# A batched matrix product on one core: leaner engine programs, and loads with wider source runs

## The chip, the cores and the metric

One core of a Trainium2 chip. Times are device microseconds (us). A profile is one further look at one execution, with its own time.

## The reference

```python
batch, m, k, n = 16, 512, 768, 1024
x: (batch, k, m) float32;  y: (batch, k, n) float32
out = np.einsum('bkm,bkn->bmn', x, y).astype(np.float32)
```

Each batch reads 1.5 MiB of x and 3 MiB of y and writes 2 MiB. Over 16 batches that is 109 MB (millions of bytes).

## The kernel before

SP issues all transfers from one queue. Two input buffers (`xs`, `ys`) alternate; VectorE (DVE) casts them to bf16, TensorE (PE) multiplies, ScalarE (ACT) moves PSUM to one of five output buffers, and SP stores with a lag of four batches. What lets a load start:

```python
    LAG = 4
    NO = 5
    # ... buffers, semaphores ...
    @block.sync
    def _(sync):
        def store(b):
            sync.wait_ge(outs, b + 1)
            sync.dma_start(o_v[b], ob[b % NO][:]).then_inc(so[b % NO], 16)

        for b in range(B):
            i = b % 2
            if b >= 2:
                sync.wait_ge(cast, b - 1)          # casts of batch b-2 are done
            sync.dma_start(xs[i][:], x_v[b]).then_inc(sx[i], 16)
            sync.dma_start(ys[i][:], y_v[b]).then_inc(sy[i], 16)
            if b >= LAG:
                store(b - LAG)
        # ... the last four stores, waits for all stores ...

    @block.vector
    def _(vector):
        for b in range(B):
            # ... wait for xs, cast x; wait for ys, cast y in two halves ...
            vector.drain().then_inc(cast, 1)

    def batch(tensor, i, first):                   # PE, cut
        for mo in range(MT):                       # MT = 4, 12 matmuls each
            tensor.wait_ge(room, 1).then_inc(room, -1)
            # ... matmuls into ps[mo]; before the 4th of them: wait for y's second half
            mm.then_inc(groups, 1)
    # ACT: one copy per mo (128 x 1024), a drain per batch that counts `outs`
```

## Time and profile before

| | before |
|---|---|
| median of runs | 262.83 us (262.77 to 262.95) |
| span of the profile | 261.2 us |
| DMA engines' busy share | 98.1% |
| PE busy | 72% |

The page, the start of the timeline and the tail are shown in the prediction. DMA issues (KB each, then median us from issue to landing):

```profile
ys<-in_y_dram SPq DMA_DIRECT2D x16, 3072.0 KB, 27.7
out_dram<-ob SPq DMA_DIRECT2D x16, 2048.0 KB, 32.1
xs<-in_x_dram SPq DMA_DIRECT2D x16, 1536.0 KB, 20.8
```

A load of x takes 20.8 us to land although its bytes need only 3.7 (3.66 us from the median engine's end of the transfer before to its end of this one): the rest is time in the queue behind other transfers. That reading is a median over 16 loads. The waits of the SP queue (total, times, longest):

```profile
SPq L72 <- DVEq L94: 188.5, 14, 15.5
```

SP spends most of its time, 188.5 of 261.2 us, waiting for the casts before it may issue a load. That alone says nothing of a loss: the DMA engines are busy for 98.1% of the span all the same.

### The profile page before, as it was taken

To read this page: it belongs to the slowest core of one execution; us is meant where nothing else is said; L and a number is where in the kernel's file an instruction comes from. 1 tells how busy PE (TensorE), PEld (TensorE's weight loads), DVE (VectorE), ACT (ScalarE), POOL (GpSimd) and SP (SyncE) were. 2 spreads that over 40 slices of the span, in tenths; PEclk is the share of its full clock that TensorE was granted. 3 is DMA by queue.
4 is the path that set the end of the run, shared out by engine and by line. 5 is a ranking of instruction groups with operands and counts; after the bars stand their busy time and mean duration, and the time that the engine had idled before them with its cause. 6 is when DMAs were issued, how large, how long until landed. Compare 5 with 4: busy or idle time off the path is not lost. (4 is left out here: it accounts for less than half of the span.)

```text
span 261.2 us, 1938 instructions
## 1 busy us (share of the span) xinstructions
PE 188.0 (72%) x768; PEld 87.1 (33%) x768; DVE 83.0 (32%) x48; ACT 66.1 (25%) x65; POOL 0.2 (0%) x4
## 2 busy tenths in 40 slices
PE   0039999998948949398595997939678394896920
PEld 0014555443513515144152342514334142342500
DVE  0261734435223252322524214252132523225000
ACT  1003343433331314114032140412314033131410
POOL 0000000000000000000000000000000000000000
PEclk9999999999986999979798697997999899797995
DMA  7999999999999999999999999999999999999993
GB/s 265 431 425 427 438 411 453 425 386 418 446 420 439 420 430 446 415 441 420 439 437 412 447 423 440 415 432 442 423 434 420 435 433 423 440 433 421 434 421 141
DMA packets 6915, 109.09 MB, mean 418 GB/s; under 512 B 768, under 2 KB 768, under 8 KB 768
## 3 DMA queue, kind: packets, MB, share of 16 engines
q1 hardware_dynamic: 6912, 109.05, 98.1%
q8 instruction: 1, 0.02, 0.0%
q14 instruction: 2, 0.02, 0.0%
HBM read 75.50 MB, written 33.55 MB: 417 GB/s over the span
## 5 line engine op out<-in xcount | busy, mean ns | idle before, releaser
L105 PE MATMUL ps<-yb,xb 128*128 128x512 bf16 x768 | 188.0, 406 | 61.6 <-PEq L100 55.9
L105 PEld LDWEIGHTS ps<-yb,xb 128*128 128x128 bf16 x768 | 87.1, 116 | 162.1 <-issue 96.7
L125 ACT COPY ob<-ps 128x1024 f32<-128x1024 f32 x64 | 64.9, 1013 | 183.6 <-PE ps L105 183.6
L93 DVE CAST yb<-ys 128x3072 bf16<-128x3072 f32 x32 | 54.9, 1757 | 88.4 <-DMA ys<-in_y_dram 88.4
L89 DVE CAST xb<-xs 128x3072 bf16<-128x3072 f32 x16 | 28.2, 1760 | 67.5 <-DMA xs<-in_x_dram 66.8
L125 ACT ACT_TABLE_LOAD x1 | 1.3, 1283 | 1.0 <-SPq L44 1.0
L142 POOL MEMSET const-uint8-127<- 128x1 uint8 x1 | 0.1, 102 | 0.0
L142 POOL MEMSET const-bfloat16-1.0<- 128x1 bf16 x1 | 0.1, 101 | 0.0
L142 POOL MEMSET const-float32-0.0<- 128x1 f32 x1 | 0.1, 98 | 0.2 <-issue 0.2
L142 POOL MEMSET const-float32-1.0<- 128x1 f32 x1 | 0.1, 98 | 0.0
## 6 DMA issues: line engine op xcount, KB each, us to landing
ys<-in_y_dram SPq DMA_DIRECT2D x16, 3072.0 KB, 27.7
out_dram<-ob SPq DMA_DIRECT2D x16, 2048.0 KB, 32.1
xs<-in_x_dram SPq DMA_DIRECT2D x16, 1536.0 KB, 20.8
```

Source lines behind the costliest of these rows:

```text
L89: nc.vector.tensor_copy(xb[i][:], xs[i][:]).then_inc(ready, 1)
L93: nc.vector.tensor_copy(yb[i][:, ks], ys[i][:, ks]).then_inc(ready, 1)
L105: mm = nc.tensor.matmul(ps[mo][:, nt], x_w[:, kt, mo], yb[i][:, kt, nt * NF:(nt + 1) * NF], start=(kt == 0), stop=(kt == KT - 1))
L125: nc.scalar.copy(ob[b % NO][:, mo].rearrange("p (t f) -> p t f", f=NF), ps[mo][:]).then_inc(room, 1)
L142: nc = _bacc.Bacc("TRN2", target_bir_lowering=False, num_devices=1)
```

## The change

Its intent: fewer instructions and barriers (no block construct, half the ACT copies, no drains per batch, `head_slot` set for PE's loop), and fewer read pieces in the loads: 32 source runs of 48 KB instead of 128 of 12 KB for x, 64 of 48 KB instead of 128 of 24 KB for y. To do without the casts' drain, loads wait for PE's groups instead.

```diff
-            if b >= 2:
-                sync.wait_ge(cast, b - 1)
-            sync.dma_start(xs[i][:], x_v[b]).then_inc(sx[i], 16)
-            sync.dma_start(ys[i][:], y_v[b]).then_inc(sy[i], 16)
+        if b >= 2:
+            nc.sync.wait_ge(groups, 2 * (b - 2) + 1)
+        wide_dma("x", xs[i][:], x_v[b], 4, True).then_inc(sx[i], 16)
+        wide_dma("y", ys[i][:], y_v[b], 2, True).then_inc(sy[i], 16)
...
-            vector.drain().then_inc(cast, 1)
...
-            sync.wait_ge(outs, b + 1)
+        if b < B - 2:
+            nc.sync.wait_ge(groups, 2 * (b + 2))
+        else:
+            nc.sync.wait_ge(outs, b - (B - 3))
...
-        for mo in range(MT):
+        for g in range(2):
             tensor.wait_ge(room, 1).then_inc(room, -1)
+            for m in range(HB):
...
             mm.then_inc(groups, 1)
...
-        with tensor.Fori(0, B // 2):
+    with nc.Fori(0, B // 2, engines=OrderedEngineSet([pe]), head_slot={pe: 0}):
...
-            for mo in range(MT):
-                nc.scalar.copy(ob[...][:, mo], ps[mo][:]).then_inc(room, 1)
-            scalar.drain().then_inc(outs, 1)
+        for g in range(2):
+            cp = nc.scalar.copy(ob[...][:, g * HB:(g + 1) * HB], ps[g][:])
+            if b < B - 1:
+                cp.then_inc(room, 1)
```

`groups` now counts half batches, two per batch, so a load of batch b waits until PE has done the first half of batch b-2.

More of the change, by code (lines that the diff above doesn't have):

```diff
@@ L3 @@
 _os.environ.setdefault("NEURON_RT_ULTRASERVER_MODE", "4")
+import copy as _copy
 from contextlib import ExitStack
@@ L10 @@
 from concourse._compat import with_exitstack
+from concourse.ordered_engine_set import OrderedEngineSet
 @with_exitstack
@@ L41 @@
     KH = KT // 2
-    GP = NT * NF
     ctx.enter_context(tc.tile_critical())
@@ L50 @@
     ob = [ec(nc.sbuf_tensor(f"ob{i}", [P, MT, N], FP32)) for i in range(NO)]
-    ps = [ec(nc.psum_tensor(f"ps{i}", [P, NT, NF], FP32)) for i in range(MT)]
+    HB = MT // 2
+    ps = [ec(nc.psum_tensor(f"ps{i}", [P, HB, NT, NF], FP32)) for i in range(2)]
     sx = [ec(nc.semaphore(f"sx{i}")) for i in range(2)]
@@ L54 @@
     so = [ec(nc.semaphore(f"so{i}")) for i in range(NO)]
-    cast = ec(nc.semaphore("cast"))
     ready = ec(nc.semaphore("ready"))
@@ L59 @@
     outs = ec(nc.semaphore("outs"))
-    block = ec(nc.Block())
-    @block.sync
-    def _(sync):
-        def store(b):
-            sync.wait_ge(outs, b + 1)
-            sync.dma_start(o_v[b], ob[b % NO][:]).then_inc(so[b % NO], 16)
-        for b in range(B):
-            i = b % 2
-            if b >= 2:
-                sync.wait_ge(cast, b - 1)
-            sync.dma_start(xs[i][:], x_v[b]).then_inc(sx[i], 16)
-            sync.dma_start(ys[i][:], y_v[b]).then_inc(sy[i], 16)
-            if b >= LAG:
-                store(b - LAG)
-        for b in range(B - LAG, B):
-            store(b)
-        for i in range(NO):
-            sync.wait_ge(so[i], 16 * len(range(i, B, NO)))
@@ L81, in _ @@
-    @block.vector
-    def _(vector):
-        for b in range(B):
-            i = b % 2
-            n = 16 * (b // 2 + 1)
-            if b >= 2:
-                vector.wait_ge(groups, MT * (b - 1))
-            vector.wait_ge(sx[i], n)
-            nc.vector.tensor_copy(xb[i][:], xs[i][:]).then_inc(ready, 1)
-            vector.wait_ge(sy[i], n)
-            for h in range(2):
-                ks = slice(h * KH, (h + 1) * KH)
-                nc.vector.tensor_copy(yb[i][:, ks], ys[i][:, ks]).then_inc(ready, 1)
-            vector.drain().then_inc(cast, 1)
@@ L96, in batch @@
-    def batch(tensor, i, first):
-        x_w = xb[i][:].rearrange("p k (j mo) -> p k mo j", mo=MT)
-        tensor.wait_ge(ready, 2).then_inc(ready, -2)
-        for mo in range(MT):
-            tensor.wait_ge(room, 1).then_inc(room, -1)
-            for nt in range(NT):
-                for kt in range(KT):
-                    if mo == 0 and nt == 0 and kt == KH:
-                        tensor.wait_ge(ready, 1).then_inc(ready, -1)
-                    mm = nc.tensor.matmul(
-                        ps[mo][:, nt], x_w[:, kt, mo],
-                        yb[i][:, kt, nt * NF:(nt + 1) * NF],
-                        start=(kt == 0), stop=(kt == KT - 1))
-            mm.then_inc(groups, 1)
@@ L111, in _ @@
-    @block.tensor
-    def _(tensor):
-        with tensor.Fori(0, B // 2):
-            batch(tensor, 0, False)
-            batch(tensor, 1, False)
-    @block.scalar
-    def _(scalar):
-        nc.scalar.nop().then_inc(room, MT)
-        for b in range(B):
-            for mo in range(MT):
-                if mo == 0 and b >= NO:
-                    scalar.wait_ge(so[b % NO], 16 * (b // NO))
-                scalar.wait_ge(groups, MT * b + mo + 1)
-                nc.scalar.copy(ob[b % NO][:, mo].rearrange("p (t f) -> p t f", f=NF),
-                               ps[mo][:]).then_inc(room, 1)
-            scalar.drain().then_inc(outs, 1)
+    made = {}
@@ new lines, in wide_dma @@
+    def wide_dma(key, dst, src, dram_rows, load):
+        if key not in made:
+            made[key] = nc.sync.dma_start(dst, src)
+            return made[key]
+        pat = mybir.BassSymbolicTensorAccessPattern
+        widen = lambda a: a.rearrange("(q r) k m -> q (r k m)", r=dram_rows)
+        plain = lambda a: a.rearrange("p k m -> p (k m)")
+        s, d = (widen(src), plain(dst)) if load else (plain(src), widen(dst))
+        return nc.sync.add_instruction(_copy.replace(
+            made[key].ins, name=nc.get_next_instruction_name(),
+            ins=(pat(ap=s.ap, dtype=s.dtype, bass_ap=s, is_dma=False),),
+            outs=(pat(ap=d.ap, dtype=d.dtype, bass_ap=d, is_dma=False),),
+            sync_info=None, ant_dge_precooked=False))
@@ new lines, in store @@
+    def store(b):
+        if b < B - 2:
+            nc.sync.wait_ge(groups, 2 * (b + 2))
+        else:
+            nc.sync.wait_ge(outs, b - (B - 3))
+        nc.sync.dma_start(o_v[b], ob[b % NO][:]).then_inc(so[b % NO], 16)
+    for b in range(B):
+        i = b % 2
+        if b >= 2:
+            nc.sync.wait_ge(groups, 2 * (b - 2) + 1)
+        wide_dma("x", xs[i][:], x_v[b], 4, True).then_inc(sx[i], 16)
+        wide_dma("y", ys[i][:], y_v[b], 2, True).then_inc(sy[i], 16)
+        if b >= LAG:
+            store(b - LAG)
@@ new lines, with batch @@
+    for b in range(B - LAG, B):
+        store(b)
+    for b in range(B):
+        i = b % 2
+        n = 16 * (b // 2 + 1)
+        if b >= 2:
+            nc.vector.wait_ge(groups, 2 * (b - 1))
+        nc.vector.wait_ge(sx[i], n)
+        nc.vector.tensor_copy(xb[i][:], xs[i][:]).then_inc(ready, 1)
+        nc.vector.wait_ge(sy[i], n)
+        for h in range(2):
+            ks = slice(h * KH, (h + 1) * KH)
+            nc.vector.tensor_copy(yb[i][:, ks], ys[i][:, ks]).then_inc(ready, 1)
+    def batch(i):
+        x_w = xb[i][:].rearrange("p k (j mo) -> p k mo j", mo=MT)
+        nc.tensor.wait_ge(ready, 2).then_inc(ready, -2)
+        for g in range(2):
+            nc.tensor.wait_ge(room, 1).then_inc(room, -1)
+            for m in range(HB):
+                for nt in range(NT):
+                    for kt in range(KT):
+                        if g == 0 and m == 0 and nt == 0 and kt == KH:
+                            nc.tensor.wait_ge(ready, 1).then_inc(ready, -1)
+                        mm = nc.tensor.matmul(
+                            ps[g][:, m, nt], x_w[:, kt, g * HB + m],
+                            yb[i][:, kt, nt * NF:(nt + 1) * NF],
+                            start=(kt == 0), stop=(kt == KT - 1))
+            mm.then_inc(groups, 1)
@@ new lines @@
+    pe = nc.tensor.engine
+    with nc.Fori(0, B // 2, engines=OrderedEngineSet([pe]), head_slot={pe: 0}):
+        batch(0)
+        batch(1)
+    nc.scalar.nop().then_inc(room, 2)
+    for b in range(B):
+        if b >= NO:
+            nc.scalar.wait_ge(so[b % NO], 16 * (b // NO))
+        for g in range(2):
+            nc.scalar.wait_ge(groups, 2 * b + g + 1)
+            cp = nc.scalar.copy(ob[b % NO][:, g * HB:(g + 1) * HB].rearrange("p m (t f) -> p m t f", f=NF),
+                                ps[g][:])
+            if b < B - 1:
+                cp.then_inc(room, 1)
+        if b == B - 2:
+            nc.scalar.drain().then_inc(outs, 1)
@@ L131 @@
+    cp.then_inc(outs, 1)
+    for i in range(NO):
+        nc.sync.wait_ge(so[i], 16 * len(range(i, B, NO)))
 _INS = ['x', 'y']
```

## The prediction

> **What bounds the kernel now.** I read the page first (busy shares, slices, DMA queues), then the timeline at the start and the end, the waits of the SP queue, fine windows over the tail, and last the single packet records of the trace.
>
> The page of the kernel before:
>
> ```profile
> span 261.2 us, 1938 instructions
> ...
> PE 188.0 (72%) x768; PEld 87.1 (33%) x768; DVE 83.0 (32%) x48; ACT 66.1 (25%) x65; POOL 0.2 (0%) x4
> ...
> DMA  7999999999999999999999999999999999999993
> ...
> q1 hardware_dynamic: 6912, 109.05, 98.1%
> q8 instruction: 1, 0.02, 0.0%
> q14 instruction: 2, 0.02, 0.0%
> ```
>
> No compute engine is above 72%, while the DMA row is 9 in every slice but the first and the last: 109.05 MB run through 16 engines that are busy 98.1% of the span. The kernel is bound by transfers from end to end; only the start, the tail, and dry spots in the queue can move the time.[...]
>
> The timeline, start:
>
> ```profile
> 0.94 0.38 SPq L72 DMA_DIRECT2D xs<-in_x_dram  x1
> ...
> 18.49 0.33 SPq L72 DMA_DIRECT2D xs<-in_x_dram  x1
> ...
> 25.00 1.01 ACT L125 COPY ob<-ps 128x1024 f32<-128x1024 f32 x1 [1.57 <-PE ps L105]
> 25.99 3.43 DVE L93 CAST yb<-ys 128x3072 bf16<-128x3072 f32 x2 [5.55 <-DMA ys<-in_y_dram]
> ```
>
> Loads of batch 2 are issued at 18.49 us, right after the casts of batch 0. The ACT copy at 25.00 is the second of batch 0: PE finishes half a batch just before it. Load 1 ends only about then (its y is seen at 25.99).
>
> Windows over the tail (columns: stretch, length, then PE, PEld, DVE, ACT, POOL busy, clock, DMA share, GB/s):
>
> ```profile
> 256.00:257.00 1.00, 0.00 (x0) 0.00 (x0) 0.00 (x0) 0.00 (x0) 0.00 (x0) 0.50 0.54 229
> 257.00:258.00 1.00, 0.00 (x0) 0.00 (x0) 0.00 (x0) 0.00 (x0) 0.00 (x0) 0.50 0.08 33
> 258.00:259.00 1.00, 0.00 (x0) 0.00 (x0) 0.00 (x0) 0.00 (x0) 0.00 (x0) 0.50 0.12 49
> 259.00:260.00 1.00, 0.00 (x0) 0.00 (x0) 0.00 (x0) 0.00 (x0) 0.00 (x0) 0.50 0.00 0
> ```
>
> Most engines are done before 257; a share of 0.08 to 0.12 is one or two of 16. The packet records say the same: of the 16 completion packets of the last store the median ends at 256.82, the last at 259.42. So one late engine sets the end, 2.6 us behind the median. Followed back by the completion packets of each transfer, the last engine is 0.75 us behind the median until about 35 us and 1.98 behind from 39 us: an instruction packet of 16 KB lies at 38.0 us and takes 1.07 us. A second engine, 1.9 late at the end, fell behind at 105 and 137 us, where no instruction packet lies.
>
> [...]median packets are 460 ns for 12 KB, 611 for 16 KB, 912 for 24 KB; 12,288 bytes more cost 452 ns, so 27.2 GB/s an engine, 435 for 16.[...] the line through those medians leaves 8 ns per packet, and successive packets overlap by about 4, so some 4 ns net.[...] here the cast of the last y starts at 235.57, although the median engine finished it at 232.45 and the last at 235.09.[...]
>
> **The change part by part.**
>
> 1. Wider source runs. Reads of x go from 128 runs of 12 KB to 32 of 48 KB, reads of y from 128 of 24 KB to 64 of 48 KB (first x and first y stay plain). The bytes, the writes and the order stay. Per engine and batch x falls from 8 read pieces to 2 and y from 8 to 4: 10 fewer. If the fixed cost goes with the read, 10 x 4 ns x 15 batches = 0.6 us; at the full 8 ns 1.2 us; if it goes with the write, nothing. I take -0.4. It can't be more: all data at 435 GB/s needs 250.6 us, and the packets without their stalls 252.7 already (254.3 of medians less 1.6 of overlap).
>
> 2. No block construct. At the start SP goes through a branch at 0.79 before its first DMA at 0.94: about -0.1. At the end SP passes its last wait at 259.80, and the block's barrier of all engines ends at 260.18, before the outer exit begins: about -0.4. Sum -0.5.
>
> 3. Fewer instructions. ACT copies go from 64 to 32, 32 per-batch drains become one[...]. If the 16 KB packet at 38 us goes or falls where it does no harm, the latest engine becomes the second latest: 2.6 to 1.9, so -0.7. I count -0.5.
>
> 4. Load waits. A load of batch b waited for the casts of batch b-2; now it waits for PE to finish half of batch b-2, about 5 to 7 us later. In steady state nothing comes of it: a load issued at 18.49, or every 15.8 us later on, has 20 us or more to landing (page: 20.8 for x, 27.7 for y), so the queue stays 10 us deep or more. But once it is too late: load 2 must wait for half of batch 0, 25.00 us instead of 18.49. The engines finish load 1 at 24.3 (first), 24.76 (median), 25.5 (last), by their completion packets. From issue to first data takes 1.0 us (0.94 to 1.95), so first data at 26.0, 25.9 with the earlier start; and the first packets out of an empty queue took 0.96 to 1.74 us instead of 0.46, 0.8 more in the mean. The median engine loses 1.1 + 0.8 = 1.9 us, the last one about 1.2. Load 3 (half of batch 1, 35.4, data at 36.4) meets a queue busy until about 26.7 + 10.9 = 37.6, and load 4 (45.7, data 46.7) one busy until 48.5: no second dry spot, and from there the stores deepen it. The pause also lines the engines up again, which takes back perhaps 0.5 of the lag. Net +1.3.
>
> 5. Stores wait for a later batch's PE groups: before store b-4, SP has already waited for a later count, so it is free. The one copy of 2,048 columns instead of two of 1,024 (1.01 us each) ends the last eviction about 0.9 us later. The last store was issued at 250.78 against a median end of the store before at 251.93; now it comes after it, so early engines wait about 0.6. The late engine, with two to three packets left, does not. From its y landing the late engine has five stores left, 5 x 4.87 = 24.3 us; the chain cast, PE, copy, issue, store is 0.5 + 2.1 + 12.05 + 1.9 + 0.9 + 4.9 = 22.4. About 2 us of slack: +0.1.
>
> Sum: -0.4 - 0.5 - 0.5 + 1.3 + 0.1 = 0.0. A second way, by the median engine: 256.82 - 0.1 - 0.4 + 1.9 = 258.2, plus a lag of 1.3 (restart spread, about half a microsecond at 55 to 58 us where all engines stall, and the stalls at 105 and 137) is 259.5, against 259.42; then 0.4 less to leave: 0.3 us faster.
>
> **Rivals.**
> - Transfers gain all they can: the wide reads save 1.2 us and smooth the stalls, and no instruction packet hits an engine (-1.5), with a mild dry spot (+0.5). Then about 260. For it: engines do stall on their own (28 packets of y at 55 to 58 us took over 1 us).[...]
> - The dry spot bites twice (loads 2 and 3), or a restart costs more than at the start: 264 to 265. For it: load 3 has only 1.2 us to spare. Against: each pause gives the next load that much more room.
> - The wide loads run badly[...]. One extra wait of 0.1 us per wide load would be 3 us over 30 loads, 266. Nothing in the trace speaks for it; both 32 and 64 divide evenly over 16.
> - Compute becomes the bound: PE is at 72%, with 55.9 us idle for inputs; two halves of PSUM give a copy of about 1.9 us a window of 5.2. No.
>
> **Range and chances.** The two sums give 0.0 and -0.3 us. The gains are more likely undersized than the loss, since someone tuned for them, so I put 261.8 us, and 259.6 to 264.2 for 8 in 10, where the ends are the first and the second rival. Over 2% faster means below 257.6, which asks that nearly all stalls vanish[...]: 0.05. Over 2% slower, above 268.1, needs the third rival: 0.04. Within 2%: 0.91.
>
> **What would show it.** Step 1: fewer packets of 48 KB, 1,816 ns each, in place of 12 and 24 KB ones; or the same counts and medians, then nothing saved. Step 2: the last landing lies about 1.4 instead of 1.8 us before the end of the span. Step 3: no instruction packet mid-run, and a late engine under 2 us behind. Step 4: SP issues load 2 at about 25 us, and the windows from 24 to 27 us show the DMA share fall, with no later dip of that kind. Step 5: the last store's issue about 0.9 us further after PE's end. I am wrong if the DMA dip is absent, if dips recur at each load, or if the steady stretch from 60 to 250 us (430 GB/s in a window over it) moves by more than 1%.

## The result, and the profile after

Over six fast runs of each on the same chips, the changed kernel took 265.99 us (265.04 to 266.88) and the kernel before 263.04 (262.77 to 263.68). A ratio is the mean time of one kernel's fast runs over that of the other's of the same rounds, so it is not quite the ratio of these medians. It is 1.0109, with a 95% interval of 1.0081 to 1.0137. So the change is 1.1% slower: within 2%, but 1.8 us outside the predicted range of 259.6 to 264.2.

The page after:

```profile
span 264.5 us, 1831 instructions
...
DMA  7996999997999999899999999999898999999975
...
q1 hardware_dynamic: 4512, 109.05, 97.1%
q8 instruction: 1, 0.02, 0.0%
q14 instruction: 1, 0.01, 0.0%
```

The bytes are the same and the packets fell from 6,912 to 4,512, as asked for. But the DMA row has a 6 in its fourth slice, about 20 to 26 us, and a 7 and a 5 at the end. The instruction packet of 16 KB is still there.

The timeline after, start:

```profile
25.16 0.47 SPq L70 DMA_DIRECT2D xs<-in_x_dram  x1
...
35.52 0.47 SPq L70 DMA_DIRECT2D xs<-in_x_dram  x1
...
47.30 0.47 SPq L70 DMA_DIRECT2D xs<-in_x_dram  x1
```

Loads 2, 3 and 4 are issued at 25.16, 35.52 and 47.30 us; the kernel before issued them at 18.49 (shown in the prediction), 29.50 and 40.49:

```profile
29.50 0.33 SPq L72 DMA_DIRECT2D xs<-in_x_dram  x1
...
40.49 0.33 SPq L72 DMA_DIRECT2D xs<-in_x_dram  x1
```

ACT's copies of the first half batches start at the same moments as these loads (25.16, 35.52 and 47.31 us): each load goes out when PE finishes a half batch.

Windows of 1 us at that place, first the kernel before, then the changed one (columns as in the prediction; a packet's bytes are counted where it starts, so single windows swing):

```profile
24.00:25.00 1.00, 1.00 (x6) 0.51 (x5) 0.00 (x0) 0.00 (x1) 0.00 (x0) 1.00 0.72 307
25.00:26.00 1.00, 1.00 (x6) 0.57 (x5) 0.01 (x1) 1.00 (x1) 0.00 (x0) 1.00 1.07 455
26.00:27.00 1.00, 1.00 (x7) 0.49 (x5) 1.00 (x1) 0.01 (x1) 0.00 (x0) 1.00 1.06 455
```

```profile
24.00:25.00 1.00, 1.00 (x7) 0.49 (x5) 0.00 (x0) 0.00 (x0) 0.00 (x0) 1.00 0.13 49
25.00:26.00 1.00, 1.00 (x6) 0.53 (x5) 0.00 (x0) 0.84 (x1) 0.00 (x0) 1.00 0.00 0
26.00:27.00 1.00, 1.00 (x6) 0.55 (x5) 0.00 (x0) 1.00 (x1) 0.00 (x0) 1.00 1.20 393
```

Before, 307 to 455 GB/s flow throughout. After, one window has 49 and the next has none: the queue has run dry. PE is busy for 1.00 of 1.00 us in both, and it is no help: it is not what sets the pace.

The DMA issues after:

```profile
ys<-in_y_dram SPq DMA_DIRECT2D x16, 3072.0 KB, 21.1
out_dram<-ob SPq DMA_DIRECT2D x16, 2048.0 KB, 25.4
xs<-in_x_dram SPq DMA_DIRECT2D x16, 1536.0 KB, 14.4
```

Landing is 6.4 to 6.7 us sooner after issue, not because transfers are faster, but because they are issued that much later. The queue has become shallower all along the run. Whether that costs anything outside the start is a question for the experiments.

The trace has 16 completion packets of 4 bytes for each transfer, one per DMA engine (768 for 48 transfers in each of the two profiles). The median engine's completion, transfer by transfer, splits the profile's difference, which is 3.50 us at the last byte (259.41 to 262.91):

| stretch | changed minus before, us |
|---|---|
| up to the end of load 1 | -0.11 |
| load 2 (dry queue) | +2.53 |
| load 3, x of load 4 | +0.22 |
| y of load 4 (a stall just before the first store) | +0.85 |
| the eleven batches after that, to the last store but one | -0.18 |
| lag of the last engine behind the median there (the last store then takes it 4.86 us in both) | +0.19 |
| **sum, last byte** | **+3.50** |
| from last byte to end of span | -0.23 |

All of the loss is in the first 62 us. The long middle is 0.18 us shorter.

### The profile page after: what moved, and what is told of

It is laid out like the page before. It is cut to its first block, busy times and chain, and to the rows that moved or that the text cites. A ratio compares the mean times of both kernels' runs of the same rounds, so it can differ in the third digit from the quotient of the medians.

```text
span 264.5 us, 1831 instructions
## 1 busy us (share of the span) xinstructions
PE 191.9 (73%) x768; PEld 87.8 (33%) x768; DVE 83.0 (31%) x48; ACT 61.1 (23%) x33; POOL 0.2 (0%) x4
## 3 DMA queue, kind: packets, MB, share of 16 engines
q1 hardware_dynamic: 4512, 109.05, 97.1%
## 5 line engine op out<-in xcount | busy, mean ns | idle before, releaser
L128 PE MATMUL ps<-yb,xb 128*128 128x512 bf16 x768 | 191.9, 412 | 62.3 <-PEq L122 54.7
L146 ACT COPY ob<-ps 128x2048 f32<-128x2048 f32 x32 | 59.8, 1869 | 194.1 <-PE ps L128 194.1
## 6 DMA issues: line engine op xcount, KB each, us to landing
out_dram<-ob SPq DMA_DIRECT2D x16, 2048.0 KB, 25.4
```

Of the source, the lines that this page charges most:

```text
L128: mm = nc.tensor.matmul(ps[g][:, m, nt], x_w[:, kt, g * HB + m], yb[i][:, kt, nt * NF:(nt + 1) * NF], start=(kt == 0), stop=(kt == KT - 1))
L146: cp = nc.scalar.copy(ob[b % NO][:, g * HB:(g + 1) * HB].rearrange("p m (t f) -> p m t f", f=NF), ps[g][:])
```

## The experiments

All theories concern the loss of 2.9 us. The main one: the late load waits empty the queue at the start. Rivals: the wide runs, the lean program with its moved instruction packet, or later effects of the shallow queue.

### One part undone, one part alone

`a_early` is the changed kernel with the old load wait put back:

```diff
-            nc.sync.wait_ge(groups, 2 * (b - 2) + 1)
+            nc.sync.wait_ge(cast, b - 1)
...
+        nc.vector.drain().then_inc(cast, 1)      # after the casts of a batch
```

> The changed kernel, but with the loads of batch b waiting again for the casts of batch b-2 (vector drain, own semaphore); all else of the change stays. Theory (the late load waits cost the time: a dry DMA queue at 24.5 to 27 us, 2.5 us for the median engine, and the stalls after it): the dry spot is gone, and the time falls from 266.0 to 262 to 263.3. Rival (the wide loads run badly): 265 or more stays. Second rival (the instruction packet at 4 us makes one engine late from the start, which the dry spot had hidden): no dry spot, but the late engine is 2.5 us or more behind at the end and the time is 263.3 to 264.5.

262.84 us against 262.81 for the kernel before, ratio 0.9998 (0.9985 to 1.0011). The whole loss is gone, within some 0.35 us. Its timeline:

```profile
19.75 0.47 SPq L71 DMA_DIRECT2D xs<-in_x_dram  x1
```

Load 2 is 5.00 us ahead of the end of load 1 (24.75 us on the median engine), and costs nothing. Nothing else in the change makes it slower, nor measurably faster.

`a_narrow` is the changed kernel with plain loads:

```diff
-        wide_dma("x", xs[i][:], x_v[b], 4, True).then_inc(sx[i], 16)
-        wide_dma("y", ys[i][:], y_v[b], 2, True).then_inc(sy[i], 16)
+        nc.sync.dma_start(xs[i][:], x_v[b]).then_inc(sx[i], 16)
+        nc.sync.dma_start(ys[i][:], y_v[b]).then_inc(sy[i], 16)
```

> The changed kernel with all loads plain (128 source runs, as before); the late waits stay. Theory (late waits are the cost): the dry spot at 24.5 to 27 us stays at about 2 to 2.6 us, and the time is 265 to 266.5. Rival (wide packets make the first packets of a refill and the stall before the first store longer, 1.5 against 0.6 us): 264 to 265, with the stall near 58 us back at 0.6 us per engine.

266.36 us (264.96 to 267.24), ratio 1.0133. The loss stays without wide loads. The stall near 58 us stays large too, 1.2 us, so the rival fails on both counts.

`b_late` is the kernel before with the late wait alone:

```diff
-                sync.wait_ge(cast, b - 1)
+                sync.wait_ge(groups, MT * (b - 2) + 2)
```

> The kernel before with one edit: the loads of batch b wait for PE to finish half of batch b-2. Theory: this edit alone gives the dry spot and most of the slowdown, +2 to +3 us, 265 to 266. Rival (wide loads or the rest of the change cost the time): 263 to 263.8.

266.60 us (265.60 to 266.81), ratio 1.0132 (1.0114 to 1.0150): one line makes the whole loss, a little more than expected. Its loss is spread otherwise, as its timeline shows:

```profile
24.12 0.33 SPq L72 DMA_DIRECT2D xs<-in_x_dram  x1
...
34.48 0.33 SPq L72 DMA_DIRECT2D xs<-in_x_dram  x1
...
47.78 0.33 SPq L72 DMA_DIRECT2D xs<-in_x_dram  x1
```

Against queue ends of 24.77, 36.92 and 48.27 us these have leads (time from the issue to the end of what was queued) of 0.65, 2.45 and 0.48 us, and x of these loads ends 1.23, 0.41 and 1.47 us later than its bytes need. I had expected one dry spot, at load 2.

`b_wide` is the kernel before with the wide loads alone (the helper of the change, the same waits):

```diff
-            sync.dma_start(xs[i][:], x_v[b]).then_inc(sx[i], 16)
-            sync.dma_start(ys[i][:], y_v[b]).then_inc(sy[i], 16)
+            wide_dma("x", xs[i][:], x_v[b], 4).then_inc(sx[i], 16)
+            wide_dma("y", ys[i][:], y_v[b], 2).then_inc(sy[i], 16)
```

> The kernel before with one edit: wide source runs of the loads (48 KB) from the second load on. Theory: the wide runs save 0.2 us by the packet medians and cost nothing: 262.5 to 263.3, the stall near 56 us stays about 0.6 us per engine. Rival (wide runs lengthen that stall to 1.5 us): 263.5 to 264.3.

262.73 us, ratio 0.9999 (0.9986 to 1.0012). Wide loads neither help nor harm in the time. In the packets they save little: one of 48 KB took 1,824 ns in the median here (1,819 in the changed kernel), against 4 x 460 = 1,840 or 2 x 912 = 1,824. Packets overlap by about 4 ns each (eight of 460 ns and a completion of 9 ns make 3.69 us, and the median engine takes 3.66), which leaves no saving at all by this reckoning. The trace says the same: over the eleven steady batches this run gained 0.01 us on the median engine, and `a_narrow`, the changed kernel without wide loads, 0.00. So the 0.18 us of the table is not shown to come from the wide loads; `a_early` has 0.10 there, and single profiles differ by as much.

### How much lead a load needs

If a load costs time only when it is issued too late before the queue ends, then the wait's place should act like a dial. Three settings of the kernel before (in short, not the diffs themselves):

```diff
 b_late5:   late wait only for b >= 5, wait for the casts for b = 2, 3, 4
 b_late1:   sync.wait_ge(groups, MT * (b - 2) + 1)      # first quarter of PE's batch
 b_late3:   sync.wait_ge(groups, MT * (b - 2) + 3)      # three quarters
```

> The kernel before with the late load wait (half of PE's batch b-2), but only from batch 5 on; loads 2, 3 and 4 keep the wait for the casts. Theory (a load costs time only where it is issued less than about 2 us before the queue ahead of it ends, which happens only at loads 2, 3 and 4, before any store has been queued): no cost, 262.6 to 263.2. Rival (each late issue costs a little, through shallower read-ahead all along the run): 264 to 266.

263.06 us against 262.92, ratio 1.0005 (0.9991 to 1.0019). Late waits from batch 5 on cost nothing, although nearly all loads have them. Shallow is not empty.

> The kernel before with the load wait on the first quarter of PE's batch b-2 (one PSUM group of 4). Theory (cost = 2.0 us less the lead over the end of the queue): load 2 is issued at about 22.4 against a queue that ends at 24.77, lead 2.4, loads 3 and 4 have 3 or more: cost 0 to 0.4 us in all, 262.8 to 263.3. Rival (any move to PE's groups costs, or a smooth dependence on the lead): 264 to 265.

262.68 us, ratio 0.9987 (0.9972 to 1.0003): no cost. PE was early in this profile, so load 2 had 3.53 us of lead rather than 2.4.

> The kernel before with the load wait on three quarters of PE's batch b-2. Theory: load 2 is issued at about 27.0 to 27.6, 2.3 to 2.8 us after the queue ends, cost 4.3 to 4.8; load 3 has about 2 to 2.6 us of lead, cost 0 to 0.4; load 4 is late again[...], cost 1.5 to 4; from load 5 on nothing. In all 6 to 9 us, 269 to 272. Rival (the cost saturates at what one refill costs, 2.5 us a load): under 267.

272.75 us (272.50 to 273.60), 3.7% slower, just above the expected range. Its timeline:

```profile
27.68 0.33 SPq L72 DMA_DIRECT2D xs<-in_x_dram  x1
...
55.45 0.33 SPq L72 DMA_DIRECT2D xs<-in_x_dram  x1
```

Load 2 comes 2.91 us after the queue ended and costs 4.80; load 4 comes 3.56 us after and costs 5.50. So the cost did not saturate, up to the 5.50 us measured here.

Over the profiles, with the lead counted from the issue to the median engine's end of the transfer before, and the cost as the time by which the median engine's x runs over its 3.66 us:

| lead, us | cost, us | where |
|---|---|---|
| 6.3 and 5.0 | 0.0 | load 2, before and `a_early` |
| 3.53 | 0.13 | load 2, `b_late1` |
| 2.65 | 0.28 | load 3, after |
| 2.45 | 0.41 | load 3, `b_late` |
| 2.07 | 0.02 | load 4, after |
| 0.65 | 1.23 | load 2, `b_late` |
| 0.48 | 1.47 | load 4, `b_late` |
| -0.49 | 2.56 | load 2, after |
| -2.91 | 4.80 | load 2, `b_late3` |
| -3.56 | 5.50 | load 4, `b_late3` |

The other late loads, lead first, are `a_narrow` (-0.70, 2.56), `a_first` (-2.15, 4.30), `a_nohead` (-0.04, 2.12 and 0.17, 2.15), `a_warm` (-1.01, 3.17 and 1.50, 0.76), `b_late3on` (0.99, 1.38) and `b_late4on` (1.52, 0.40). Over all of them, below a lead of about 1 us the cost is 1.9 to 2.4 us less the lead. Between 1.5 and 3 us it is 0 to 0.8 with scatter. This is the cost to the median engine; the time follows the last engine and can rise by less.

### Which loads, and why more than one

`b_late3on` and `b_late4on` are the kernel before with the late wait from load 3 or 4 on:

```diff
+                if b < 3:                         # 4 in b_late4on
                     sync.wait_ge(cast, b - 1)
+                else:
+                    sync.wait_ge(groups, MT * (b - 2) + 2)
```

> The kernel before with the late wait from load 3 on; load 2 keeps the wait for the cast. By the law of the lead: load 3 issued at 34.5 to 35.4 against a queue that ends at 35.75, lead 0.3 to 1.3, cost 0.7 to 1.7; then load 4 at 45.2 to 46.5 against 47.5 to 48.4, lead about 2, cost 0 to 0.5; the first-store stall perhaps 0.4 more. Time 263.6 to 265.2. Rival (only load 2 matters): 262.6 to 263.3.

263.78 us, ratio 1.0034 (1.0019 to 1.0049). Load 3 had a lead of 0.99 and cost 1.38, load 4 had 2.94 and cost 0.71, more than expected, and the first-store stall was gone instead of larger. The expected range holds, but by luck in part: the median engine was 1.7 us later at the last store but one, and the time rose by only 0.9, because the last engine's lag behind it fell from 2.6 to 1.5 us.

> The kernel before with the late wait from load 4 on. By the law: load 4 issued at about 45.2 to 45.7 against a queue that ends at 46.7, lead 1 to 1.5, cost 0.5 to 1.0. Time 263.3 to 264.2. Rival (load 4 was late only because the loads before it were): 262.6 to 263.2.

263.75 us, ratio 1.0032 (1.0017 to 1.0046). Load 4 had a lead of 1.52 and cost 0.40, less than expected; about as much again came from the stall behind it, 1.5 us where the kernel before has 0.7. So no single load carries the loss: each of the three can be late as the first one, and when all are late the whole is 3.5 us.

Two experiments tried to make load 2 less late. `a_nohead` is the changed kernel without `head_slot`:

```diff
-    with nc.Fori(0, B // 2, engines=OrderedEngineSet([pe]), head_slot={pe: 0}):
+    with nc.Fori(0, B // 2, engines=OrderedEngineSet([pe])):
```

> The changed kernel[...]. The 16 KB packet should move from 4 to about 37 us, y of batch 0 arrive 1.3 us earlier, and load 2 be issued at 23.9 to 25.2 instead of 25.2 to 26.7. Theory A (the lateness at load 2 is simply passed on): about 1 us faster than the changed kernel, 264.6 to 265.4. Theory B (a closed loop: what load 2 loses less, load 4 loses more, as in the run of the kernel before with late waits, 1.2 + 0.4 + 1.5 us): no gain, 265.6 to 266.8.

267.99 us (265.67 to 268.31), ratio 1.0162: slower than both theories said. The packet did move, from 4.2 to 38.6 us, and the first y's cast started at 14.92 instead of 16.12 us. But the first half batch was done at 24.81, hardly earlier than 25.16, since this time PE needed 9.89 us from the cast to the half, not 9.04; load 2 still cost 2.12, and load 4, with a lead of 0.17, now cost 2.15 as well. The runs fall in two clusters, 265.7 to 266.1 and 267.9 to 268.3, so one profile (268.31 us, of the slower cluster) does not describe them all.

`a_warm` is the changed kernel with 64 matmuls of zeros ahead of PE's loop:

```diff
+    nc.tensor.wait_ge(zero, 1)                    # a small tile of zeros is written
+    for _ in range(64):
+        nc.tensor.matmul(ps[1][:, 0, 0], wz[:, 0:P], wz[:], start=True, stop=True)
```

> The changed kernel with 64 dummy matmuls of zeros on PE ahead of its loop[...]; nothing waits for them. Theory (load 2 is late by PE's slow first matmuls, 6 to 12 of them at 427 ns instead of 216[...]): half of batch 0 is done at about 24.0 instead of 25.2 to 26.7, load 2 costs 1.2 to 1.5 instead of 2.6 to 4.0, the runs spread under 1 us, and the time is 264 to 265.3. Rival (closed loop through load 4): 265.3 to 266.5 with a small spread.

266.03 us (265.65 to 266.10), ratio 1.0113. The rival holds: the runs spread only 0.45 us, but the time stays. The timeline, ACT's first copies:

```profile
23.16 1.87 ACT L152 COPY ob<-ps 128x2048 f32<-128x2048 f32 x1 [20.91 <-PE ps L131]
...
37.35 1.87 ACT L152 COPY ob<-ps 128x2048 f32<-128x2048 f32 x1 [7.15 <-PE ps L131]
```

The first half batch was done 2 us earlier than in the changed kernel (23.16 against 25.16), and load 2 cost only 0.76. But the edit changed two things. The first y's cast, here and then in the changed kernel:

```profile
14.85 3.43 DVE L118 CAST yb<-ys 128x3072 bf16<-128x3072 f32 x2 [5.53 <-DMA ys<-in_y_dram]
```

```profile
16.12 3.43 DVE L115 CAST yb<-ys 128x3072 bf16<-128x3072 f32 x2 [5.54 <-DMA ys<-in_y_dram]
```

Of the 2 us, 1.27 is this earlier y, for the extra matmuls also moved the 16 KB packet from 4.2 to 18.0 us; only 0.73 is the faster start of PE (8.31 us from cast to half instead of 9.04). PE then finished batch 0 early, idled for the next y, started that batch slowly again (granted clock 0.50 from 31.6 to 35.0 us), and half of batch 1, 10.0 us after its cast, came at 37.35 instead of 35.52. Load 3 was 1.01 us after the queue's end and cost 3.17.

That is a closed loop, and its length is in the traces. From the start of a y cast to half a batch done is 8.31 us when PE is free and its granted clock 1.00 (39.00 to 47.31 in the changed kernel), up to 10.4 when it starts slow or is still at the batch before. Then about 2.0 us until the load runs, 10.95 for its bytes, and 0.9 to 2.9 from the median engine's end to the start of the cast, which waits for the last engine (in the changed kernel the first y ends at 13.78 us on the median engine and 15.65 on the last, and its cast starts at 16.12): 22 to 26 us from the y of batch b-2 to the y of batch b. Measured from cast to cast it was 22.9 and 23.9 in the changed kernel, 24.8 and 24.7 in `b_late`, 25.8 and 25.6 in `a_nohead`. With two buffers that is the time for two batches. While only loads are in the queue, a batch takes 10.97 us (y casts at 14.99, 25.99 and 36.99 in the kernel before), two 22.0. At 22 to 26 us the loop is as long as the queue can bear or longer, so a slow start of PE shows up as lost time. With stores, a batch takes 15.8 us, two 31.6, and the loop has 5 to 9 us to spare, which is why `b_late5` is free. With the cast's wait the 8.3 us become 3.5 (14.99 to 18.49 in the kernel before), and the loop is free from the start.

The number of slow matmuls at the start varies: over seventeen profiles 6 to 12 of the first matmuls were slow, most of them 427 ns apart instead of 216; `a_warm` had none in its first batch. The spacing drops to 216 where a trace's first clock record (granted clock 1.00) begins, at 22.05 us in the kernel before and 21.22 in the changed one. In the kernel before no load waits for these slow matmuls. Where load 2 has the late wait it does: those kernels' runs spread by 1.1 to 2.6 us (`a_warm` 0.45), while `a_early`, `b_wide`, `b_late5` and `b_first` spread by 0.4 to 0.6. That the number of slow matmuls makes the spread is the author's estimate from these spreads; it is not shown run by run, since only one run of each was traced.

### The stall before the first store

In the kernel before, all engines pause for 0.6 us in all at 55 to 58 us, at the end of load 4 and just ahead of the first store: packets of y are slow there from 55.4 us on, and the store's first packet starts at 57.84. In the changed kernel this took 0.85 us more. Two experiments ask what it belongs to.

`b_lag3` is the kernel before with a shorter lag of the stores:

```diff
-    LAG = 4
+    LAG = 3
```

> The kernel before with stores lagging the loads by 3 batches instead of 4, so that the first store stands behind the loads of batch 3. For the stall of all 16 engines at 55 to 58 us (0.6 to 0.7 us per engine), which stood just before the first store in every profile so far, and was larger (1.0 to 1.5) in those with late loads. Theory A (it belongs to the first store): the stall moves to the end of load 3, about 45 to 47 us. Theory B (it belongs to the time or to load 4): it stays at 55 us or at the end of load 4. Time 262.5 to 263.3 under both.

The stall moved to 44 to 47 us, the end of load 3, where the first store now stands: 303 GB/s in that window.

```profile
44.00:47.00 3.00, 3.00 (x16) 1.57 (x15) 0.01 (x1) 1.09 (x2) 0.00 (x0) 1.00 1.03 303
```

So it belongs to the first store. My time was wrong: 266.36 us, ratio 1.0123 (1.0108 to 1.0139), where I had said 262.5 to 263.3. Windows over its end show why:

```profile
251.00:253.00 2.00, 2.00 (x11) 1.06 (x10) 0.00 (x0) 1.01 (x1) 0.00 (x0) 1.00 0.46 197
253.00:255.00 2.00, 2.00 (x11) 1.08 (x10) 0.00 (x0) 1.01 (x1) 0.00 (x0) 1.00 0.04 16
255.00:257.00 2.00, 1.14 (x6) 0.35 (x4) 0.00 (x0) 0.82 (x1) 0.00 (x0) 1.00 0.00 0
```

With a lag of 3 only three stores lie between the last load and the last store, so the queue is empty for 5.9 us on the median engine and 3.5 on the last one while PE and ACT work on the last batch. The time rose by 3.4. The lag of 4 covers that chain: in the kernel before, the median engine ends the last store 4.89 us after the one before it, with no gap. It is the lead of an issue again, at the other end of the kernel.

`b_first` adds to the kernel before one small store (16 rows of 512 B, overwritten later) behind the first four loads:

```diff
+            if b == 1:
+                sync.wait_ge(zero, 1)             # tz, [16, 128], is written
+                sync.dma_start(o_v[B - 1][0:16, 0, 0:128], tz[:]).then_inc(sz, 16)
...
+            if b == B - 1:
+                sync.wait_ge(sz, 16)              # ahead of the last store
```

> The kernel before with one added small store (16 rows of 512 B, zeros, to a part of the last output that the last store overwrites later) behind the first four loads. Theory (the stall of 0.6 to 0.7 us per engine before the first store belongs to the first write to the output): the stall moves to 20 to 26 us and is one engine-packet long, the stall at 55 us goes; since the queue is full all the time the time falls by 0 to 0.6 us: 262.2 to 262.9. Rival (it belongs to the first large store, not to the first write): the stall stays at 55 us, 262.7 to 263.3.

262.83 us, ratio 0.9997. The small store went out at 24.3 to 25.4 us, and the stall stayed at 55 us:

```profile
55.00:58.00 3.00, 3.00 (x16) 1.56 (x15) 0.00 (x0) 1.43 (x2) 0.00 (x0) 1.00 1.00 341
```

```profile
55.00:58.00 3.00, 3.00 (x16) 1.57 (x15) 0.00 (x0) 1.42 (x2) 0.00 (x0) 1.00 1.03 352
```

The first line is the kernel before, the second this run. It is not the first write as such that stalls.

`a_first` is the changed kernel with the same small store:

> The changed kernel with the same small early store. Theory: of the changed kernel's loss of 2.9 us the dry spot at load 2 (2.5 us) stays and the stall near 58 us (1.5 us per engine) goes or shrinks below 0.3: 264.6 to 265.5. Rival (the stall is not the first write): 265.7 to 266.7.

268.03 us (266.09 to 268.38), verdict unclear, 1.0174: worse than both theories. In its profile PE had 12 slow matmuls instead of 6, the first half batch was done at 26.67 instead of 25.16, and load 2 went out at 26.66 us, two after the queue's end. The run tells more of PE's slow start than of the stall.

What makes the stall larger in some runs is open. As the excess of y of load 4 over its bytes it was 0.5 to 0.8 us in the kernels with early loads, 1.2 to 1.6 in seven of those with late ones, but 0.6 in `a_warm` and 0.0 in `b_late3on`; and it was 1.05 in `b_lag3`, which has early loads.

### A version that repairs it

`a_best` ("the third run" in the text below) is the changed kernel with the cast's wait for loads 2, 3 and 4 only (three drains), the late wait from 5 on, and the small early store. `a_best_nohead` is the same without `head_slot`.

```diff
+            if b < 5:
+                nc.sync.wait_ge(cast, b - 1)
+            else:
+                nc.sync.wait_ge(groups, 2 * (b - 2) + 1)
```

> The changed kernel with the waits for the casts put back for loads 2, 3 and 4 only (three drains), late waits from load 5 on, and the small early store. Theory (only loads 2 to 4 can run the queue dry): no dry spot, the lean exit stays (0.25 us), the first-store stall is spread: 261.8 to 262.8. Rival (late waits later on still cost, or the instruction packet at 4 us decides the end): 262.8 to 263.5.

> The kernel of the third run[...]. Theory (the 16 KB instruction packet costs one engine about 1.2 us wherever it falls, so its place does not matter): the packet moves from about 4 to about 37 us, the last engine is still 2 us or more behind the median, the time is within 0.4 us of the third run. Rival (the early packet is what makes the end late): 0.5 to 1 us faster than the third run.

262.73 us, ratio 0.9991 (0.9978 to 1.0003), and 262.55 us, ratio 0.9986 (0.9972 to 0.9999). Three drains undo the loss; the early store by itself did nothing (`b_first`). The second version is perhaps 0.1% faster than the kernel before, which is all that the rest of the change is worth. The 16 KB packet moved from 4.4 to 36.3 us between the two; in both the last engine was over 2.5 us behind the median from load 4 to the last store but one. So where the packet falls makes little difference, as expected.

## Why the prediction was wrong

**What bounds the kernel** was right: transfers, from end to end; nothing in PE, DVE or ACT mattered except through when loads are issued.

**Step 1, wider runs** (-0.4 us): over-sized. The packets of 48 KB were as forecast (1,819 ns), but alone they gained 0.01 us in the steady stretch of eleven batches, where the prediction's estimate of 4 ns per read piece would give 0.44, and nothing in the time (`b_wide`). The rival that wide loads run badly was wrong as well.

**Step 2, no block** (-0.5): half of it in the span, almost none in the time. The end gained 0.23 us (1.82 to 1.59 us from last byte to end of span), but the measured time is longer than the span, by 1.98 us in the mean of the changed kernel's runs against 1.81 in those of the kernel before, so most of it was lost outside the span; the start gained nothing, since SP goes through a branch at 0.79 us in both traces: its first load is at 0.95 us instead of 0.94.

**Step 3, fewer instructions** (-0.5): failed. The packet of 16 KB did not go away. It moved to 4.2 us, and one engine is 1.1 us later in the first load than before (last engine behind the median at the end of x: 1.84 us, before 0.75). The casts of the first y start at 16.12 instead of 14.99. The last engine was again 2.8 us behind the median at the last store but one, as against 2.6.

**Step 4, load waits** (+1.3): the mechanism was right and the size wrong. This is the step that failed most: by `a_early` the waits cost the whole 2.9 us, over twice the forecast. The prediction said "The median engine loses 1.1 + 0.8 = 1.9 us"; it lost 2.56 at load 2. Its issue came at 25.16 instead of 24.9, and from issue to full flow took 2.07 us rather than 1.8. A wide load takes SP 0.47 us to issue, not 0.33, and its first data came 1.26 us after issue instead of 1.0. The prediction then said "no second dry spot". In the changed kernel's profile that nearly holds (0.28 and 0.02 us), but single runs differ: loads 3 and 4 lost 0.4 and 1.5 in `b_late`, and 0.4 and 2.2 in `a_nohead`. I had checked each load against one timeline, with PE's matmuls 216 ns apart, and had not closed the loop: here a late load makes a late y, an idle PE, a slow half batch (10.0 us in `a_warm`, not 8.31) and the next late load. And the credit of 0.5 for lining the engines up was not kept in the changed kernel, though other runs kept more (1.1 in `b_late3on`). The last engine's lag did fall from 2.1 to 0.4 us at load 2, then single engines stalled and it was 3.0 at the end of load 4.

**Missing step**: the stall before the first store, 0.85 us larger in the profile. Why is open.

**Step 5, stores and the last eviction** (+0.1): right. The last copy took 1.87 us and the last store was issued at 256.14, 0.9 us after the median engine had run dry; most engines waited, but the last one, on which the end depends, did not (it ends 4.86 us after its store before, the time of the bytes).

**The sum.** Of the 2.9 us between the sum of 0.0 and the result, about 1.6 is step 4. The other 1.3 is what steps 1 to 3 and 5 were to gain together: by `a_early`, which has them all but for the casts' drains, they gained 0.0 us in the time, give or take 0.35.

**The range.** The sum gave 0.0 and the second way -0.3, yet I put the forecast 1.0 us below the sum, on the grounds that someone must have tuned for the gains. No line of the profile said so. And the second rival, "The dry spot bites twice (loads 2 and 3), or a restart costs more than at the start: 264 to 265", is near what happened, though still 1 us short of it; the top of the range should have been above it. The class, within 2%, was right.

## What to carry to other kernels

Where a queue sets the time, as here with 98.1% busy, ask where it can run dry. What counted here was not its mean depth (late waits from batch 5 on: ratio 1.0005) but the lead of each issue over the end of what is queued (a lead under 1 us cost the median engine 1.9 to 2.4 us less the lead); look at the first batches by themselves, before stores fill the queue. When a wait is moved to a later event to save a drain, add up the whole round trip from one buffer's landing to its next (22 to 26 us here), and compare it with as many periods of the queue as there are buffers (22.0 us for two before the stores, 31.6 with them), with PE's slow start in it (6 to 12 matmuls 427 ns apart instead of 216 here). A wait that is free in the steady state may need its earlier form for the first few rounds only: here for loads 2, 3 and 4 (`a_best`, ratio 0.9991).
